# A two-layer streaming trunk on one core: the first chunk of the first layer in a fixed order on four engines

## The chip, the cores and the metric

The kernel runs on one core of one Trainium2 chip. The metric is the device time of one launch in microseconds (us), the median of the runs shown. A core has TensorE (PE in the profile: matmuls, and PEld, its weight loads), VectorE (DVE), ScalarE (ACT), GpSimd (POOL) and SyncE (SP), which here issues the loads. They run their own instruction queues in order and wait for one another by semaphores.

## The reference, cut to what matters

```python
def rmsnorm(x, w):
    x32 = x.astype(jnp.float32)
    y = x32 * lax.rsqrt(jnp.mean(x32 * x32, axis=-1, keepdims=True) + EPS)
    return (y * w.astype(jnp.float32)).astype(x.dtype)

def hybrid_layer(x, layer, norm_w, w_in, ...):
    h = rmsnorm(x, norm_w)
    proj = jnp.einsum('bld,de->ble', h, w_in)
    ...   # forgetting attention, Mamba-2 scan and differential attention on slices of proj,
    ...   # each times a gate and w_branch; merged
    return x + jnp.einsum('bld,de->ble', merged, w_out)
```

There are two layers and a final RMSNorm; x has 256 tokens of 1024 channels. The change lies in `h = rmsnorm(x, norm_w)` of the first layer and in the first 512 columns of `proj`.

## The kernel before, in words

All matrices are float32. To multiply in PE's faster fp32r format without losing precision, each operand is split into a high part (rounded to fp32r) and a low part (the rest), and a product is three matmuls: high by high, high by low, low by high. Weights come packed in chunks of 512 columns (one of 272, one of 272 with small columns); a chunk is four *units* of two 128-row blocks each (`UNITS`, `KU`). For each unit SP issues one load into a `raw` tile (four buffers, `wraw`), ACT casts it to the high part (`whi`, L231) and DVE subtracts to get the low part (`wlo`, L232); after that the raw buffer is free for the load of a later unit. `load_chunk` (L215) does this, and `prefetch` (L914) calls it chunk by chunk.

h is computed by token half `tt` (128 tokens). Squares with a sum go to ACT (L942) and DVE (L944); `norm_scale` (L206) adds four partial sums, `rstd_of` scales (DVE, L181) and raises to the power -0.5 on POOL (L183). `norm_apply` (L210) multiplies x by the token's factor and by the norm weight in one DVE instruction for each half of 512 channels, `c`; the norm weight is a row copied to all 128 partitions by two loads (`load_nwb`, `spread`, L291). `split_rows` (L195) turns h: four PE transposes (L198) put 4 blocks of 128 channels into one PSUM bank, channels now on partitions, and `split_bank` splits it two blocks at a time into `hT` high (ACT, L188) and low (DVE, L189).

`bform` (L240) is a product for one token half with 512 (or 272) output columns, 24 matmuls (L249); `aform` (matmuls L264) has the weights stationary. The first chunk is fv0: its first token half is done with an own order of matmuls, `EARLY` (L237), that takes the passes with the high weights of units 1 to 3 before the one with the low weights; its second half, the chunk fv1 and so on follow. 24 transposes of the identity (`WARM`, L930) run first.

The order of instructions on each engine is set by a planner, which simulates the program with its own costs, takes program order as priority, and puts what stands in `tc.high_priority(URGENT)` first. `tc.issue_after(ins)` puts instructions of ins's engine behind ins. In the opening the loads are issued as x's first half (two), the norm weight (two), two weight units, x's second half (two), two weight units, then the parameters of both layers. At most eight loads are out at a time in the order of issue.

Of the kernel before, what the change touches and what calls it, by code (L numbers as in the profile page):

```python
# [11 lines left out]
F32 = mybir.dt.float32  # L12
F32R = mybir.dt.float32r
# [4 lines left out]
P = 128  # L18
# [14 lines left out]
BUDGET = 3.0  # L33
URGENT = 3000
WARM = 24
BEHIND = 1
ACTSQ = (2, 4)


def rope_tables():  # L40
# [46 lines left out]
    return flat  # L87


def pack_small(conv_w, conv_b, ssm_norm_w, subln_w):  # L90
    rows = np.concatenate([conv_w.reshape(DEPTH, 64, P), conv_b.reshape(DEPTH, 16, P),
                           ssm_norm_w.reshape(DEPTH, 8, P), subln_w.reshape(DEPTH, 1, P)], axis=1)
    return np.ascontiguousarray(rows.transpose(0, 2, 1))


# [1 line left out]
def trunk(ctx: ExitStack, tc: tile.TileContext, x, norm_w, weights, small, vectors,  # L97
# [21 lines left out]
    def rows():  # L119
        return [a2([P, 512]) for _ in range(2)]  # L120
# [7 lines left out]
    def bank(pool, name):  # L128
        return pool.tile([P, 512], F32, name=name)
# [21 lines left out]
    def load_params(l):  # L151
        d = par[l]
        lam_init = 0.8 - 0.6 * math.exp(-0.3 * l)
        pT = const.tile([P, 89], F32, name=f"pT{l}")
        nc.sync.dma_start(pT, small[l])
# [56 lines left out]

    chunks, _ = chunk_list()

    def load_chunk(off, total, after=None, behind=()):  # L215
        units = []
        for u in range(UNITS):
            raw = wraw.tile([P, KU * 512], F32, name="raw")[:, 0:KU * total]
            o = off + u * KU * P * total
            ins = nc.sync.dma_start(raw, weights[o:o + KU * P * total].rearrange("(p f) -> p f", p=P)).ins  # L220
            if u == BEHIND:
                for late in behind:
                    tc.add_manual_dep(late, ins.name, mybir.DependencyInfo(
                        mybir.DependencyClass.NoSync, mybir.DependencyReason.DATA), reason="order")
            hi = wsp.tile([P, KU * 512], F32R, name="whi")[:, 0:KU * total]
            lo = wsp.tile([P, KU * 512], F32R, name="wlo")[:, 0:KU * total]
            with ExitStack() as es:
                if u > 0 and after:
                    for ins in after:
                        es.enter_context(tc.issue_after(ins))  # L230
                S.copy(out=hi, in_=raw)  # L231
                V.tensor_tensor(out=lo, in0=raw, in1=hi.bitcast(F32), op=ALU.subtract)  # L232
            units.append(tuple(t.rearrange("p (k n) -> p k n", k=KU) for t in (hi, lo)))
        return units, total

    ORDER = [(u, k, i) for u in range(UNITS) for k in range(KU) for i in range(3)]
    EARLY = [(u, k, i) for u, i in ((0, 0), (0, 1), (0, 2), (1, 0), (1, 2), (1, 1),  # L237
                                    (2, 0), (2, 2), (2, 1), (3, 0), (3, 2), (3, 1)) for k in range(KU)]

    def bform(ch, act, tt, order=ORDER):  # L240
        units, n = ch
        ahi, alo = act
        ps = bank(pp, "pp")
        for u, k, i in order:
# [4 lines left out]
            PE.matmul(ps[:, 0:n], lhsT=at(a, kt)[:, ts], rhs=w[:, k, 0:n],  # L249
                      start=((u, k, i) == order[0]), stop=((u, k, i) == order[-1]))  # L250
        return ps

    def aform(ch, act, jj):
# [31 lines left out]
    def load_nwb(l):  # L285
        L[l]["nwb"] = spread(norm_w[l])
# [624 lines left out]
    queue = list(chunks)  # L911
    loaded = []

    def prefetch(n, after=None, behind=()):  # L914
        while queue and n > 0:
            l_, k_, _, off, m = queue.pop(0)
            loaded.append((l_, k_, load_chunk(off, m, after, behind)))
            n -= 1

    constants()  # L920
    xt = [rows() for _ in range(2)]

    def load_x(tt):
        for c in range(2):
            cs = slice(512 * c, 512 * c + 512)
            yield nc.sync.dma_start(xt[tt][c], x[0, tt * P:(tt + 1) * P, cs]).ins

    warm = bank(pq, "pq")
    for i in range(WARM):
        PE.transpose(warm[:, (i % 4) * P:(i % 4 + 1) * P], ident, ident)  # L930

    list(load_x(0))
    load_nwb(0)
    x1 = list(load_x(1))
    for tt in range(2):
        xs, ss = rows(), sm.tile([P, 4], F32, name="ss")
        with tc.high_priority(URGENT):
            for q in range(4):
                qs = slice(256 * (q % 2), 256 * (q % 2) + 256)
                a, b = xs[q // 2][:, qs], xt[tt][q // 2][:, qs]  # L940
                if q < ACTSQ[tt]:
                    S.activation(out=a, in_=b, func=AF.Square, accum_out=ss[:, q:q + 1])  # L942
                else:
                    V.tensor_tensor_reduce(out=a, in0=b, in1=b, scale=1.0,  # L944
                                           scalar=0.0, op0=ALU.mult, op1=ALU.add, accum_out=ss[:, q:q + 1])
        g = make_h(0, tt, xt[tt], xs, ss, 1)
        next(g)
        if tt == 0:
            for _ in g:
                pass  # L950
            prefetch(1, [i.ins for i in L[0]["split"]], x1)
            prefetch(1)
        else:
            jobs.append([g, 1])
    for idx, it in enumerate(items):
        if it["key"] == "dq0" and it["l"] == 0:
            with tc.issue_after(L[0]["split"][0].ins), tc.issue_after(L[0]["split"][1].ins):
                load_params(1)
            nc.sync.dma_start(rot, rope_t)
        if it["pre"]:  # L960
            it["pre"]()
        l = it["l"]
        if it["wait"]:
            n = 0
            while it["wait"] not in L[l]:
                assert jobs
                pump(100.0)
                n += 1
            if n > 1:
                print("forced", l, it["key"], n)  # L970
        prefetch(it["n"])
        got = [loaded.pop(0) for _ in range(it["n"])]
        assert got[0][:2] == (l, it["key"]), (got[0][:2], it["key"])
        if idx == 0:
            ch, act = got[0][2], it["act"]()
            it["evac"][0](0, bform(ch, act, 0, EARLY))
            while "h1" not in L[0]:
                pump(BUDGET)
            it["evac"][0](1, bform(ch, act, 1))
            pump(BUDGET)  # L980
            got, it["evac"] = got[1:], it["evac"][1:]
            with tc.issue_after(L[0]["split"][0].ins), tc.issue_after(L[0]["split"][1].ins):
# [37 lines left out]
```

## Time and profile before

| | us |
|---|---|
| median of 3 runs (range) | 955.47 (955.02 to 956.32) |
| profiled execution, its own time | 956.56 |
| span of that execution | 954.8 |
| PE, PEld busy | 942.0, 843.5 |
| DVE, ACT, POOL busy | 700.9, 599.3, 36.3 |
| mean granted TensorE clock | 0.993 |

The profile shows one execution on the core. Busy time is the sum of an engine's instructions without overlaps; PE's matmuls are pipelined, so the time from one start to the next says more than the length of one. The granted clock is a share of 2.4 GHz: 1.00 or 0.50 (1.2 GHz). Idle time stands with the instruction that ended it and with what released it. L followed by a number is a line of the kernel.

### The profile page before, as it was taken

To read this page: it belongs to the slowest core of one execution; us is meant where nothing else is said; L and a number is where in the kernel's file an instruction comes from. 1 tells how busy PE (TensorE), PEld (TensorE's weight loads), DVE (VectorE), ACT (ScalarE), POOL (GpSimd) and SP (SyncE) were. 2 spreads that over 40 slices of the span, in tenths; PEclk is the share of its full clock that TensorE was granted. 3 is DMA by queue.
4 is the path that set the end of the run, shared out by engine and by line. 5 is a ranking of instruction groups with operands and counts; after the bars stand their busy time and mean duration, and the time that the engine had idled before them with its cause. 6 is when DMAs were issued, how large, how long until landed. Compare 5 with 4: busy or idle time off the path is not lost.

```text
span 954.8 us, 16246 instructions
## 1 busy us (share of the span) xinstructions
PE 942.0 (99%) x5924; PEld 843.5 (88%) x5924; DVE 700.9 (73%) x1434; ACT 599.3 (63%) x1141; POOL 36.3 (4%) x71
## 2 busy tenths in 40 slices
PE   7999999999999999999999999999999999999997
PEld 5999999988898988888889989898889999888885
DVE  5678677987667877864768768699777677797463
ACT  4668686654557868653546859566536596975442
POOL 1001100000000000100000110000000000010000
PEclk7999999999999999999999999999999999999999
DMA  6866634575555555555558664456645555555551
GB/s 231 263 219 198 206 101 166 159 226 154 177 189 181 182 190 179 151 171 194 193 181 271 209 206 134 132 172 191 201 143 194 174 186 186 188 158 162 177 188 44
DMA packets 60319, 172.45 MB, mean 181 GB/s; under 512 B 7312, under 2 KB 15824, under 8 KB 60240
## 3 DMA queue, kind: packets, MB, share of 16 engines
q1 hardware_dynamic: 60240, 171.43, 55.4%
q8 instruction: 46, 0.75, 0.3%
q14 instruction: 33, 0.27, 0.1%
HBM read 167.14 MB, written 2.16 MB: 177 GB/s over the span
## 4 chain that ended last, share of the span: by engine, by line
PE 98%; DMA 1%; DVE 1%; ACT 0%; SPq 0%; POOLq 0%; issue 0%
PE pp L249 51%; PE pp L264 34%; PE pq L400 2%; PE pt L457 2%; PE pq L583 1%; PE pq L401 1%; PE pq L447 1%; DMA raw<-in_weights_dram 1%; PE pt L627 1%; PE pt L198 1%; PE pt L458 1%; PE pq L692 1%; PE pq L590 0%; PE pt L700 0%; PE pq L499 0%; PE pt L699 0%
## 5 line engine op out<-in xcount | busy, mean ns | idle before, releaser
L249 PE MATMUL pp<-whi,a 128*128 128x512 f32 (+1 forms) x1472 | 452.5, 387 | 1.9 <-ACT a L188 1.1
L232 DVE TENSOR_TENSOR wlo<-raw,whi 128x1024 fp32r<-128x1024 f32 (+1 forms) x296 | 349.8, 1193 | 82.8 <-ACT whi L231 80.0
L231 ACT CAST whi<-raw 128x1024 fp32r<-128x1024 f32 (+1 forms) x296 | 302.2, 1027 | 135.2 <-PE pp L249 72.3
L264 PE MATMUL pp<-a,whi 128*128 128x256 f32 x1792 | 332.8, 284 | 0.0
L249 PEld LDWEIGHTS pp<-whi,a 128*128 128x128 f32 x1472 | 273.0, 189 | 55.3 <-ACT a L188 1.7
L264 PEld LDWEIGHTS pp<-a,whi 128*128 128x128 f32 x1792 | 281.5, 191 | 1.7 <-issue 1.4
L249 PE MATMUL pp<-wlo,a 128*128 128x512 f32 (+1 forms) x736 | 281.5, 385 | 0.0
L264 PE MATMUL pp<-a,wlo 128*128 128x256 f32 x896 | 255.2, 285 | 0.0
L264 PEld LDWEIGHTS pp<-a,wlo 128*128 128x128 f32 x896 | 171.5, 191 | 1.4 <-issue 1.4
L249 PEld LDWEIGHTS pp<-wlo,a 128*128 128x128 f32 x736 | 138.9, 189 | 25.8 <-DVE wlo L232 0.5
L183 POOL TENSOR_TENSOR rstd<-rstd,mhalf 128x2 f32<-128x2 f32 (+2 forms) x26 | 18.9, 727 | 760.6 <-DVE rstd L181 739.7
L473 DVE SCALAR_TENSOR_TENSOR a<-sw,pT,a 128x255 f32<-128x255 f32 (+2 forms) x96 | 41.8, 477 | 8.1 <-ACT a L470 7.9
L406 ACT ACTIVATE sc<-sc,dnm 128x128 f32<-128x128 f32 x64 | 28.6, 450 | 8.4 <-DVE dnm L403 8.3
L188 ACT CAST a<-pt 128x256 fp32r<-128x256 f32 x32 | 11.5, 371 | 33.2 <-PE pt L198 27.0
L400 PE MATMUL pq<-a,a 128*128 128x128 f32 (+1 forms) x128 | 31.8, 283 | 0.0
L809 DVE SCALAR_TENSOR_TENSOR a<-a,pp 128x512 f32<-128x512 f32 x24 | 16.4, 682 | 20.9 <-PE pp L249 20.9
L401 PE MATMUL pq<-a,a 128*128 128x128 f32 (+1 forms) x128 | 31.5, 269 | 0.0
L406 ACT ACTIVATE sc<-sc,nm 128x128 f32<-128x128 f32 (+1 forms) x64 | 28.5, 447 | 1.3 <-DVE nm L403 1.1
L400 PEld LDWEIGHTS pq<-a,a 128*128 128x128 f32 x128 | 23.7, 191 | 0.3
L401 PEld LDWEIGHTS pq<-a,a 128*128 128x128 f32 x128 | 23.6, 191 | 0.3
L403 DVE CUSTOM_DVE_ANT_0 sc<-pq,sc 128x128 f32<-128x128 f32 (+1 forms) x64 | 19.5, 351 | 5.9 <-POOL sc L426 4.9
L191 ACT ACTIVATE a<-pt,pT 128x256 fp32r<-128x256 f32 x32 | 14.9, 473 | 14.1 <-PE pt L627 12.4
(161 smaller groups left out, 842.6 us busy)
## 6 DMA issues: line engine op xcount, KB each, us to landing
raw<-in_weights_dram SPq DMA_DIRECT2D x280, 512.0 KB, 4.5
raw<-in_weights_dram SPq DMA_DIRECT2D x16, 272.0 KB, 3.5
sc<-scr SPq DMA_DIRECT2D x16, 256.0 KB, 5.5
a<-scr SPq DMA_DIRECT2D x16, 256.0 KB, 5.6
a<-in_x_dram SPq DMA_DIRECT2D x8, 256.0 KB, 5.2
sc<-scr SPq DMA_DIRECT2D x16, 128.0 KB, 5.2
a<-in_norm_w_dram SPq DMA_DIRECT2D x4, 256.0 KB, 6.5
rp<-a SPq DMA_DIRECT2D x32, 32.0 KB, 4.1
```

Of the source, the lines that this page charges most:

```text
L183: G.tensor_tensor(out=r[:, 0:width], in0=r[:, 0:width], in1=mhalf[:, 0:width], op=ALU.pow)
L231: S.copy(out=hi, in_=raw)
L232: V.tensor_tensor(out=lo, in0=raw, in1=hi.bitcast(F32), op=ALU.subtract)
L249: PE.matmul(ps[:, 0:n], lhsT=at(a, kt)[:, ts], rhs=w[:, k, 0:n], start=((u, k, i) == order[0]), stop=((u, k, i) == order[-1]))
L264: PE.matmul(ps[:, j * T:(j + 1) * T], lhsT=w[:, k, c0:c0 + P], rhs=at(a, kt), start=(kt == 0 and j == 0 and i == 0), stop=(kt == KT - 1 an ...
L400: PE.matmul(ps[:, o:o + n], lhsT=q[:, j, qs], rhs=k[:, j, 0:n], start=True, stop=False)
L401: PE.matmul(ps[:, o:o + n], lhsT=q[:, j, qs], rhs=kl[:, j, 0:n], start=False, stop=True)
L403: V.tensor_tensor_reduce(out=sc[:, sl], in0=ps[:, sl], in1=bias[:, sl], scale=-0.125, scalar=BIG, op0=ALU.add, op1=ALU.min, accum_out=nm[: ...
L406: S.activation(out=sc[:, sl], in_=sc[:, sl], func=AF.Exp, scale=-1.0, bias=nm[:, t:t + 1], accum_out=rs[:, t:t + 1])
L457: PE.matmul(po[r, 0:T], lhsT=v0, rhs=pTs[i][:, 0:T], start=True, stop=False)
L473: V.scalar_tensor_tensor(out=xc[:, s:T], in0=u[:, 0:T - s], scalar=pr["conv"](j, k), in1=xc[:, s:T], op0=ALU.mult, op1=ALU.add)
L809: V.scalar_tensor_tensor(out=t, in0=t, scalar=1.0, in1=ps, op0=ALU.add, op1=ALU.mult)
```

## The change

The opening is written out in one function, `opening()`, inside `tc.manual_schedule` for PE, ACT, DVE and SP, which keeps program order on these four queues instead of the planner's. In it:

- The norm weight of the first layer comes as `wcol`, 8 values per partition (channel on partition), packed behind the small parameters. The two row loads are gone for the first layer; the second layer is as before.
- The loads are issued as x's first half, `wcol`, weight units 0 and 1, x's second half, units 2 and 3.
- The multiplication of x takes the token's factor alone: on DVE for the first token half, on POOL and ACT (512 channels each) for the second, whose four squares are all on ACT.
- `split_k` splits the turned h by blocks of 128 channels and multiplies by `wcol` there: high on ACT (on DVE for the first two blocks), low on DVE.
- Splits of weight units, h blocks and the matmuls of fv0's first token half are interleaved unit by unit. PE gets 8 (`FILL`) and three times 4 (`HOLD`) more transposes of the identity between them.
- The parameters and the second chunk's casts and subtractions stand behind the last split of the second token half. `load_chunk` is cut into three helpers; the `EARLY` order and the manual dependence of loads go.

The core of the diff:

```diff
+    def opening():
+        _, _, _, off, n = queue.pop(0)
...
+        def split_k(tt, ps, k, hi_on=S):
+            pk, ts = ps[k // 4][:, k % 4 * P:(k % 4 + 1) * P], slice(tt * P, (tt + 1) * P)
+            h, o, w = at(hT[0], k)[:, ts], at(hT[1], k)[:, ts], wcol[:, k:k + 1]
+            if hi_on is S:
+                hi = S.activation(out=h, in_=pk, func=AF.Copy, scale=w)
+            else:
+                hi = V.tensor_scalar(out=h, in0=pk, scalar1=w, scalar2=None, op0=ALU.mult)
+            lo = V.scalar_tensor_tensor(out=o, in0=pk, scalar=w, in1=h.bitcast(F32),
+                                        op0=ALU.mult, op1=ALU.subtract)
+            return hi.ins, lo.ins
+
+        def passes(u, *forms):
+            for i in forms:
+                for k in range(KU):
+                    kt = u * KU + k
+                    a, w = ((0, his), (0, los), (1, his))[i]
+                    PE.matmul(first, lhsT=at(hT[a], kt)[:, 0:P], rhs=per_k(w[u])[:, k, :],
+                              start=(u == 0 and i == 0 and k == 0), stop=(u == 3 and i == 1 and k == 1))
...
+            load_x(0)
+            nc.sync.dma_start(wcol, small[0, :, 89:97])
+            raw = [load_raw(off, n, u) for u in range(2)]
+            load_x(1)
+            raw += [load_raw(off, n, u) for u in range(2, 4)]
+            keep_warm(WARM)
             for q in range(4):
+                square(0, q, q < 2)
+            r = norm_scale(ss[0])
+            p0 = []
+            for c in range(2):
+                V.tensor_scalar(out=xs[0][c], in0=xt[0][c], scalar1=r[:, 0:1], scalar2=None, op0=ALU.mult)
+                p0.append(turn(0, c))
+            keep_warm(FILL)
+            his[0] = split_hi(raw[0], n)
+            for k in (0, 1):
+                split_k(0, p0, k, V)
+            passes(0, 0, 2)
+            keep_warm(HOLD)
+            los[0] = split_lo(raw[0], his[0], n)
+            for k in (2, 3):
+                split_k(0, p0, k)
+            his[1] = split_hi(raw[1], n)
+            passes(1, 0, 2)
+            keep_warm(HOLD)
+            los[1] = split_lo(raw[1], his[1], n)
+            passes(0, 1)
+            for k in (4, 5):
+                split_k(0, p0, k)
+            for q in range(4):
+                square(1, q, True)
+            his[2] = split_hi(raw[2], n)
+            r = norm_scale(ss[1])
+            passes(2, 0, 2)
+            keep_warm(HOLD)
+            los[2] = split_lo(raw[2], his[2], n)
+            passes(1, 1)
+            for k in (6, 7):
+                split_k(0, p0, k)
+            his[3] = split_hi(raw[3], n)
+            G.tensor_scalar(out=xs[1][0], in0=xt[1][0], scalar1=r[:, 0:1], scalar2=None, op0=ALU.mult)
+            S.activation(out=xs[1][1], in_=xt[1][1], func=AF.Copy, scale=r[:, 0:1])
+            passes(3, 0, 2)
+            los[3] = split_lo(raw[3], his[3], n)
+            passes(2, 1)
+            p1 = [turn(1, 0)]
+            passes(3, 1)
+            p1.append(turn(1, 1))
+            for k in range(8):
+                tail = split_k(1, p1, k)
...
+            it["evac"][0](0, ps0)
+            it["evac"][0](1, bform(ch0, it["act"](), 1))
+            it["n"], it["evac"] = it["n"] - 1, it["evac"][1:]
+            with tc.issue_after(tail[0]), tc.issue_after(tail[1]):
+                prefetch(it["n"])
                 load_params(0)
```

## Rows read from the trace of the kernel before

**Rows 1.** The page, part 4: the chain that ended last, by engine.

```profile
...
PE 98%; DMA 1%; DVE 1%; ACT 0%; SPq 0%; POOLq 0%; issue 0%
...
```

**Rows 2.** Busy time by engine, TensorE clock granted, DMA share, GB/s, 23 to 940 us.

```profile
...
23.00:940.00 917.00, 917.00 (x5828) 824.02 (x5827) 685.52 (x1404) 584.99 (x1107) 32.79 (x55) 1.00 0.56 181
...
```

**Rows 3.** Chain of waits in order of time, 0 to 60 us: start, length, what.

```profile
...
2.65 7.64 DMA raw<-in_weights_dram
...
22.70 18.28 PE pp L249 x122
...
```

**Rows 4.** Timeline of the opening: start, length, engine, line, operation, count, idle before.

```profile
...
1.70 0.91 SPq L291 DMA_DIRECT2D a<-in_norm_w_dram  x2
...
4.45 0.43 DVE L944 CUSTOM_DVE_ANT_0 a<-a 128x256 f32<-128x256 f32 x1 [4.45 <-DMA a<-in_x_dram]
...
6.81 0.75 DVE L210 SCALAR_TENSOR_TENSOR a<-a,rstd,a 128x512 f32<-128x512 f32 x1 [1.13 <-DMA a<-in_norm_w_dram]
...
9.05 0.75 DVE L210 SCALAR_TENSOR_TENSOR a<-a,rstd,a 128x512 f32<-128x512 f32 x1 [1.49 <-DMA a<-in_norm_w_dram]
...
14.44 1.99 ACT L231 CAST whi<-raw 128x1024 fp32r<-128x1024 f32 x2
...
15.52 2.36 DVE L232 TENSOR_TENSOR wlo<-raw,whi 128x1024 fp32r<-128x1024 f32 x2 [0.52 <-ACT whi L231]
...
```

**Rows 5.** Stretches of the opening, columns as in rows 2.

```profile
...
4.00:4.50 0.50, 0.50 (x4) 0.50 (x4) 0.05 (x1) 0.50 (x3) 0.00 (x0) 1.00 0.54 180
7.00:9.50 2.50, 0.83 (x6) 0.42 (x4) 1.01 (x2) 0.00 (x0) 0.00 (x0) 1.00 0.91 370
10.50:11.00 0.50, 0.12 (x1) 0.00 (x0) 0.00 (x0) 0.50 (x1) 0.00 (x0) 0.50 1.08 430
17.00:20.50 3.50, 3.50 (x10) 2.73 (x9) 2.60 (x6) 3.17 (x9) 0.56 (x1) 0.50 0.59 164
20.50:21.00 0.50, 0.50 (x4) 0.41 (x3) 0.50 (x2) 0.01 (x1) 0.00 (x0) 0.98 0.03 9
...
```

**Rows 6.** Timeline of TensorE: transposes at 2 and 22 us, matmuls at 440 us.

```profile
...
2.03 5.18 PE L930 MATMUL pq<-ident 128*128 128x128 f32 x24 [2.03 <-POOL mhalf L147]
...
21.64 1.03 PE L198 MATMUL pt<-ident,a 128*128 128x128 f32 x8
...
439.96 0.39 PE L249 MATMUL pp<-wlo,a 128*128 128x512 f32 x1
440.19 0.61 PE L249 MATMUL pp<-whi,a 128*128 128x512 f32 x2
...
```

**Rows 7.** Groups by line and shape: count, busy us, mean ns; last, min/median/max ns.

```profile
...
L232 DVE TENSOR_TENSOR wlo<-raw,whi 128x544 fp32r<-128x544 f32 x16 | 11.3, 722 | 7.5 <-ACT whi L231 7.5
...
L707 DVE SCALAR_TENSOR_TENSOR a<-pt,rstd,a 128x128 f32<-128x128 f32 x32 | 9.7, 344 | 5.3 <-POOL rstd L183 5.3
...
L614 DVE TENSOR_SCALAR a<-a,rstd 128x256 f32<-128x256 f32 x16 | 4.5, 348 | 2.3 <-POOL rstd L183 2.3
...
L171 DVE TENSOR_TENSOR br<-br 128x128 f32<-128x128 f32 x2 | 0.6, 282 | 0.0
...
L191 ACT ACTIVATE a<-pt,pT 128x256 fp32r<-128x256 f32 x32 | 14.9, 473 | 14.1 <-PE pt L627 12.4 <-DVE a L192 1.4
...
L183 POOL TENSOR_TENSOR rstd<-rstd,mhalf 128x4 f32<-128x4 f32 x4 | 4.1, 1018 | 325.0 <-DVE rstd L181 325.0
L183 POOL TENSOR_TENSOR rstd<-rstd,mhalf 128x1 f32<-128x1 f32 x6 | 3.3, 558 | 174.0 <-DVE rstd L181 174.0
...
masks.py:199 POOL TENSOR_SCALAR_AFFINE_SELECT ident<-ident 128x128 f32<-128x128 f32 x1 | 0.3, 298 | 0.0
...
L426 POOL TENSOR_SCALAR_AFFINE_SELECT sc<-sc x32: 403/409/1475, 70.1 to 570.2; 128x256 f32<-128x256 f32 x32
...
```

**Rows 8.** Timeline at 95 us: a select on POOL beside a weight split on DVE.

```profile
...
95.67 1.22 DVE L232 TENSOR_TENSOR wlo<-raw,whi 128x1024 fp32r<-128x1024 f32 x1
...
95.68 1.48 POOL L426 TENSOR_SCALAR_AFFINE_SELECT sc<-sc 128x256 f32<-128x256 f32 x1 [1.12 <-DMA sc<-scr]
...
```

More of the change, by code (lines that the diff above doesn't have):

```diff
@@ L213, in trunk, with load_raw, split_hi @@
     chunks, _ = chunk_list()
-    def load_chunk(off, total, after=None, behind=()):
+    def load_raw(off, total, u):
+        raw = wraw.tile([P, KU * 512], F32, name="raw")[:, 0:KU * total]
+        o = off + u * KU * P * total
+        nc.sync.dma_start(raw, weights[o:o + KU * P * total].rearrange("(p f) -> p f", p=P))
+        return raw
+    def split_hi(raw, total):
+        hi = wsp.tile([P, KU * 512], F32R, name="whi")[:, 0:KU * total]
+        S.copy(out=hi, in_=raw)
+        return hi
@@ L221, in load_chunk @@
[L221 to L232, printed above, removed]
@@ L240, in bform @@
-    def bform(ch, act, tt, order=ORDER):
+    def bform(ch, act, tt):
         units, n = ch
@@ L243, in bform @@
         ps = bank(pp, "pp")
-        for u, k, i in order:
+        for u, k, i in ORDER:
             whi, wlo = units[u]
@@ L912, in trunk, with prefetch @@
     loaded = []
-    def prefetch(n, after=None, behind=()):
+    def prefetch(n):
         while queue and n > 0:
             l_, k_, _, off, m = queue.pop(0)
-            loaded.append((l_, k_, load_chunk(off, m, after, behind)))
+            loaded.append((l_, k_, load_chunk(off, m)))
             n -= 1
     constants()
[L921 to L937, printed above, removed]
-            for q in range(4):
[L939 to L954, printed above, removed]
+    def opening():
+        _, _, _, off, n = queue.pop(0)
+        st = L[0]
+        xt = [rows() for _ in range(2)]
+        xs = [rows() for _ in range(2)]
+        ss = [sm.tile([P, 4], F32, name="ss") for _ in range(2)]
+        hT = st["hT"] = halves()
+        wcol = const.tile([P, 8], F32, name="wcol")
+        warm = bank(pq, "pq")
+        first = bank(pp, "pp")
+        def keep_warm(m):
+            for i in range(m):
+                PE.transpose(warm[:, (i % 4) * P:(i % 4 + 1) * P], ident, ident)
+        def load_x(tt):
+            for c in range(2):
+                nc.sync.dma_start(xt[tt][c], x[0, tt * P:(tt + 1) * P, 512 * c:512 * c + 512])
+        def square(tt, q, on_act):
+            qs = slice(256 * (q % 2), 256 * (q % 2) + 256)
+            a, b = xs[tt][q // 2][:, qs], xt[tt][q // 2][:, qs]
+            if on_act:
+                S.activation(out=a, in_=b, func=AF.Square, accum_out=ss[tt][:, q:q + 1])
+            else:
+                V.tensor_tensor_reduce(out=a, in0=b, in1=b, scale=1.0,
+                                       scalar=0.0, op0=ALU.mult, op1=ALU.add, accum_out=ss[tt][:, q:q + 1])
+        def turn(tt, c):
+            ps = bank(pt, "pt")
+            for j in range(4):
+                PE.transpose(ps[:, j * P:(j + 1) * P], xs[tt][c][:, j * P:(j + 1) * P], ident)
+            return ps
+        def split_k(tt, ps, k, hi_on=S):
[3 more added lines that the diff above has]
+                hi = S.activation(out=h, in_=pk, func=AF.Copy, scale=w)
+            else:
+                hi = V.tensor_scalar(out=h, in0=pk, scalar1=w, scalar2=None, op0=ALU.mult)
[9 more added lines that the diff above has]
+                              start=(u == 0 and i == 0 and k == 0), stop=(u == 3 and i == 1 and k == 1))
+        his, los, r = {}, {}, {}
+        with tc.manual_schedule(engines={mybir.EngineType.PE, mybir.EngineType.Activation,
+                                         mybir.EngineType.DVE, mybir.EngineType.SP}):
+            load_x(0)
[4 more added lines that the diff above has]
+            keep_warm(WARM)
+            for q in range(4):
+                square(0, q, q < 2)
+            r = norm_scale(ss[0])
+            p0 = []
+            for c in range(2):
+                V.tensor_scalar(out=xs[0][c], in0=xt[0][c], scalar1=r[:, 0:1], scalar2=None, op0=ALU.mult)
[37 more added lines that the diff above has]
+                tail = split_k(1, p1, k)
+        st["h0"] = st["h1"] = True
+        return ([(per_k(his[u]), per_k(los[u])) for u in range(UNITS)], n), first, tail
@@ L970, in trunk @@
                 print("forced", l, it["key"], n)
-        prefetch(it["n"])
-        got = [loaded.pop(0) for _ in range(it["n"])]
-        assert got[0][:2] == (l, it["key"]), (got[0][:2], it["key"])
         if idx == 0:
[L975 to L982, printed above, removed]
-                load_params(0)
+            it["evac"][0](0, ps0)
+            it["evac"][0](1, bform(ch0, it["act"](), 1))
+            it["n"], it["evac"] = it["n"] - 1, it["evac"][1:]
+            with tc.issue_after(tail[0]), tc.issue_after(tail[1]):
+                prefetch(it["n"])
+                load_params(0)
+            got = [loaded.pop(0) for _ in range(it["n"])]
+        else:
+            prefetch(it["n"])
+            got = [loaded.pop(0) for _ in range(it["n"])]
+            assert got[0][:2] == (l, it["key"]), (got[0][:2], it["key"])
         for s in range(2):
```

32 lines of the change are left out of this document (18 added, 14 removed).

## The prediction

> **What bounds the kernel now.** I read the chain of waits first, then busy time by stretch, then the timeline of the first 24 us. The chain is TensorE (PE) for 98% [rows 1]: the kernel is one long queue of matmuls. From 23 to 940 us PE is busy in all of the 917 us and at the full clock, while VectorE (DVE, 685 us) and ScalarE (ACT, 585 us) have slack [rows 2]. So nothing is to be had there; what can move is the moment from which PE has no more gaps. In the chain in order of time that moment is the hand-over at 22.70 us, the first matmul of the second token half; before it the chain is a DMA until 10.29 us (2.65 + 7.64) and then short pieces of ACT, DVE and PE [rows 3]. Everything PE does after the hand-over is the same in both kernels: 24 matmuls of fv0 for the second token half and all later chunks. The sum is therefore 22.70 minus the new hand-over, and whether PE stays without gaps after it.
>
> Why is the hand-over so late? Two reasons. First the loads: the two norm-weight loads (each 256 KB, one row copied to 128 partitions) are issued at 1.70 us, ahead of the weights. DVE waits for them twice, until 6.81 and 9.05 us [rows 4], and while they run the DMA engines move 180 GB/s, against 430 later [rows 5]. Second the clock. The 24 warm-up transposes take 5.18 us, 0.21 apart, although the clock column already reads 1.00 there; eight transposes at 21.6 us take 1.03 us, 0.11 apart [rows 6]. So the full clock came only near the end of the warm-up. Then PE works 0.83 us of the 2.5 from 7.0 to 9.5, the clock falls to 0.50 by 10.5, and it is back at 20.5 us, after PE was busy for all of 17.0 to 20.5 [rows 5]. Most of the 24 matmuls of the first token half so ran at 1.2 GHz: 512 columns in 0.43 us, against 0.23 from start to start at the full clock [rows 6].
>
> **The change part by part.** I carry the four queues forward by hand. Back to back, the next start comes some 0.08 us before an end: two DVE weight splits of 1.22 us [rows 8] take 2.36 together, two ACT casts 1.99 [rows 4]. So I count 1.14 and 0.95 each, and 0.08 more for the last.
>
> *Loads.* x's first half is issued and lands as before, 4.45 us [rows 4]. The per-channel weights (4 KB, 32 bytes a partition) follow; no row shows so small a load. It costs between 0 and 2.2 us (a norm-weight half: 6.81 to 9.05); I take 0.1, since by bytes it is 1/64 of that half, and nothing waits for it before 7.7. Without the two slow loads a weight unit (0.52 MB) needs 1.25 us at 420 GB/s: unit 0 at 5.8, unit 1 at 7.05, x's second half at 8.3, units 2 and 3 at 9.55 and 10.8. SyncE's nine issues, 0.45 us each [rows 4], end by 5 us and stay ahead. Unit 0 so comes 4.5 us earlier; the other end is 0, if it was not these loads that held the queue.
>
> *Norm of the first half.* Squares and the power on GpSimd (POOL) stay and end at 6.4 us. The multiplication by the row's norm alone costs between 0.35 us (128x256) and 0.75 (128x512 with the weight) [rows 7, 4]; I take 0.49, an estimate nearer to the first row, which is the same operation. The halves are ready at 6.9 and 7.35. The transposes stand behind the warm-up, which ends at 7.2; the banks are ready at 7.7 and 8.1. The 8 fillers run until 8.8.
>
> *Splits.* Eight casts and eight subtractions of 128x256 become 16 and 16 of 128x128 with a scale. One on DVE: 0.34 [rows 7], 0.26 apart. One on ACT: between 0.24 and 0.47 (half and all of a 128x256 with the same kind of scale) [rows 7]; I take 0.36, 0.28 apart. DVE then runs: two channel blocks, high and low, 7.7 to 8.9; unit 0's low part to 10.05; blocks 2 and 3 to 10.55; unit 1 to 11.7; blocks 4 and 5 to 12.2; two small norm steps to 12.5; unit 2 to 13.65; blocks 6 and 7 to 14.15; unit 3 to 15.3. ACT: unit 0's high part 5.8 to 6.9; blocks 2, 3 to 8.4; unit 1 to 9.35; blocks 4, 5 to 9.9; four squares (0.40 each, between the 0.36 of a block and a 0.47) to 11.4; unit 2 to 12.45; blocks 6, 7 to 13.0; unit 3 to 13.95; its half of the second norm to 14.6. By that table DVE and ACT are the bound in the opening, no longer the loads.
>
> *POOL's multiplication (128x512, new).* It starts at 13.5, after the power. Price: no multiplication on POOL is in the trace. Its selects take 0.30 for 128 columns and 0.41 for 256, so 0.63 for 512; its power takes 0.56 for one column and 1.02 for four, which for 512 would be 79 us [rows 7]. I take 0.63: a select is also one simple step per element, a power is not. A select that began beside a DVE weight split took 1.48 us instead of 0.41 [rows 8], so units 2 and 3 on DVE may hold it up; it is then done at 14.2, at the latest at about 15.6.
>
> *PE.* Unit 0's four matmuls 8.8 to 9.75, 4 fillers to 10.2; unit 1's wait for blocks 2, 3 and end at 11.1, fillers to 11.55; unit 0's low part to 12.0; unit 2 waits for ACT until 12.45. From there PE has no wait left: 4 matmuls 0.92, fillers 0.44, two 0.46, four 0.92, two 0.46, four transposes 0.44 (they need POOL's result at 15.65), two 0.46 (they need unit 3's low part, 15.3), four transposes 0.44. That is 4.54, hand-over at 17.0. Behind it the second token half is split on ACT and DVE in 0.28 us steps, while PE needs 0.69 us a block: no wait.
>
> **Sum:** 22.70 - 17.0 = 5.7 us less. The 20 fillers (2.2 us at full clock) stand where PE would wait, except the last hold (0.44), counted. What covers the rest: the second chunk (fv1) is first used 24 matmuls later, at 22.5; its loads wait in SyncE's queue for the raw buffers, which come free at 10 to 15.3 instead of from 12.6 on, and DVE and ACT are rid of the opening at 18.9. One of its units costs 0.72 us on DVE [rows 7], so unit 0 is there at about 19.6 to 21, before 22.5. If that cover fails, PE waits for the difference.
>
> The profiled execution took 956.56 us for a span of 954.8. 956.56 - 5.7 = 950.9; the median of the runs, 955.47, lies 1.1 below it, and from it the same gain gives 949.8. I cannot tell how much of that 1.1 is the opening; I take 950.3.
>
> **The rivals.** (a) *The clock is not held.* PE falls back to 1.2 GHz near 10 us as before. For: it fell in this trace with PE mostly idle before it, and was back only at 20.5 [rows 5]; the table leaves gaps too. Against: none of them is over 0.8 us, and at the lower level PE's work fills them. Price: the 4.54 us from 12.45 on take at most twice that, hand-over at 21.5 and a gain of 1.2; with the full clock back half-way 19.3, gain 3.4. I take the second: 2.3 on the forecast, 952.6.
> The fillers are transposes, and those are weighed here. In the trace nothing but transposes ran before their spacing went from 0.21 to 0.11 us [rows 6]. The Trainium skill (TensorE: Matmul & The Clock Gate, Part 4: PE-mode transpose) says that the full clock does not engage for transposes, because they do not count as busy in the same way. By that rule fillers would hold nothing and rival (a) would be the forecast; the trace does not agree with it, and (a) has the chance that the gaps of the table leave it.
>
> (b) *The gain is given back in the next chunks*, because parameter steps and evacuations on DVE go ahead of fv1's splits. The parameter steps are twelve, of at most 0.28 us [rows 7]; behind 18.9 all of them would bring unit 0 to 23.0, 0.5 late, and two evacuations of a bank to 24: up to 1.5 us of gap, 951.8. Against it: a unit takes 0.72 us on DVE and its six matmuls about as long, so it happens once, and steps that nothing waits for may go later.
>
> (c) *The loads come no earlier*: the queue was slow for another reason. Unit 0 then lands at 10.3 as before, the others 1.25 apart and unit 3 at 15.3; its cast, its low part and the last 0.9 us of PE bring the hand-over to 18.5, 1.5 late: 951.8. For: the first us of a queue may be slow for any load. Against: x, in the same slots, was there by 4.45, and the queue ran at 430 by 10.5 [rows 4, 5].
>
> (d) *Slower: POOL multiplies at the rate of its power.* The second half's first turn waits for it and PE's queue behind it: unit 3's low part, the second turn, all else. It decides from 2.1 us on (13.5 to 15.6), and from 7.8 us on the kernel is slower than before. At 0.15 us a column: 79 us, hand-over 77 later, about 1027 us. For: the only arithmetic on POOL in this trace. Against: the selects, 0.9 ns a column.
>
> (e) *The rest of the program is ordered anew* and loses a few us: it has no gaps now, so it can only lose; with DVE busy 75% [rows 2] I count up to 8 us, 958.
>
> **How the numbers follow.** Forecast 0.62, (a) 0.13, (b) 0.11, (c) 0.06, (d) 0.03, (e) 0.05. The forecast's own hand-over is 16.2 to 18.2 (a twentieth on every step, and the small load up to 1 us late), that is 949.0 to 952.0 with the 1.1 us between profile and median. The range takes in (a), (b) and (c) and an opening a little faster than the table (the loads alone, unit 3 at 10.8 and the 3.2 us behind it, allow 14): 948.2 to 953.7. Less than 0.2% (1.9 us) cannot be told from no change. Faster 0.91, same 0.04 (parts of (b) and (e)), slower 0.05.
>
> **What would show it.** Unit 0's cast on ACT starts before 6.5 us (loads). The clock reads 1.00 throughout 8 to 17 us (fillers). POOL's multiplication takes under 1 us by itself and PE's transposes of the second half do not wait for it. The 24th matmul of the first token half and the last of the turns end near 17 us, and from there PE shows no idle time; 23 to 930 looks as before. It is wrong if the hand-over is after 19 us, or if it is at 17 and the time does not fall by 5.

## The result, and the profile after

The changed kernel takes 964.25 us (median of 6 runs, 961.28 to 965.78) against 955.59 for the kernel before beside it (6 runs, 955.02 to 956.32): a ratio of 1.0085, with a 95% interval of [1.0067, 1.0103]. It is 0.85% slower; 950.3 was forecast, in a range of 948.2 to 953.7. The profiled execution took 964.85 us, with a span of 963.1.

Where that comes from is read with a ledger that the next tables use too: for a matmul of the kernel before, how much earlier (-) or later (+) the other kernel starts the matmul at which it has done the same number of columns (transposes of the identity, which fill time, are left out). After the change TensorE (PE) is 0.35 us late at 28 us, 0.97 at 55, 1.60 at 64, 6.94 at 80, 8.45 at 150 and 8.42 at 900. So the opening gained nothing, and some 7 us more went between 60 and 150 us, where [rows 2] had no gap. A ledger compares one execution of each kernel, and these lie up to 1.3 us beside the median of their kernel, so a difference of less than about 1 us between two ledgers says little.

Stretches of the kernel after (PE, PEld, DVE, ACT and POOL busy, granted clock, DMA share, GB/s). The third answers to [rows 2]:

```profile
...
10.50:11.00 0.50, 0.28 (x3) 0.04 (x1) 0.41 (x2) 0.06 (x1) 0.00 (x0) 1.00 1.01 390
17.00:20.50 3.50, 3.31 (x12) 2.27 (x12) 2.48 (x4) 1.92 (x3) 2.39 (x1) 0.65 0.31 80
...
23.00:940.00 917.00, 913.87 (x5791) 820.26 (x5790) 683.47 (x1402) 585.60 (x1103) 31.62 (x54) 1.00 0.57 181
77.00:80.00 3.00, 0.63 (x5) 0.43 (x4) 1.24 (x9) 1.13 (x5) 1.26 (x4) 0.91 0.73 220
80.00:86.30 6.30, 6.30 (x30) 6.30 (x31) 6.07 (x25) 6.30 (x20) 4.40 (x7) 0.50 0.75 250
...
```

The clock is no longer down at 10.5 as in [rows 5], but it falls at 18, for 3.4 us, and a second time at 79.5, for 6.8 us, behind a stretch in which PE worked 0.63 us of 3.

Timeline of the opening after (start, length, engine, line, operation, count, idle before and its releaser); it answers to [rows 3, 4]:

```profile
...
7.09 1.05 ACT L223 CAST whi<-raw 128x1024 fp32r<-128x1024 f32 x1 [2.74 <-DMA raw<-in_weights_dram]
...
9.43 1.22 DVE L228 TENSOR_TENSOR wlo<-raw,whi 128x1024 fp32r<-128x1024 f32 x1
9.60 0.37 ACT L963 ACTIVATE a<-pt,wcol 128x128 fp32r<-128x128 f32 x1 [1.46 <-DVE a L966]
...
10.57 0.34 DVE L966 SCALAR_TENSOR_TENSOR a<-pt,wcol,a 128x128 fp32r<-128x128 f32 x1
...
10.95 0.37 ACT L963 ACTIVATE a<-pt,wcol 128x128 fp32r<-128x128 f32 x1 [0.97 <-DVE a L966]
11.21 1.03 ACT L223 CAST whi<-raw 128x1024 fp32r<-128x1024 f32 x1
...
12.30 1.20 PE L975 MATMUL pp<-whi,a 128*128 128x512 f32 x4 [1.51 <-ACT whi L223]
...
15.66 1.03 ACT L223 CAST whi<-raw 128x1024 fp32r<-128x1024 f32 x1
...
16.86 2.53 POOL L1021 TENSOR_SCALAR a<-a,rstd 128x512 f32<-128x512 f32 x1
...
18.51 1.03 ACT L223 CAST whi<-raw 128x1024 fp32r<-128x1024 f32 x1
...
23.19 0.47 PE L252 MATMUL pp<-whi,a 128*128 128x512 f32 x1
...
24.31 0.37 ACT L963 ACTIVATE a<-pt,wcol 128x128 fp32r<-128x128 f32 x1 [0.42 <-DVE a L966]
...
24.71 0.35 DVE L966 SCALAR_TENSOR_TENSOR a<-pt,wcol,a 128x128 fp32r<-128x128 f32 x1 [0.43 <-ACT a L963]
...
25.09 0.62 ACT L963 ACTIVATE a<-pt,wcol 128x128 fp32r<-128x128 f32 x2 [0.42 <-DVE a L966]
...
27.97 2.27 ACT L223 CAST whi<-raw 128x544 fp32r<-128x544 f32 x4
...
29.12 0.72 DVE L228 TENSOR_TENSOR wlo<-raw,whi 128x544 fp32r<-128x544 f32 x1
...
```

Waits of the whole kernel after (us in total, times, longest):

```profile
...
ACT a L963 <- DVE a L966: 7.1, 9, 1.5
...
DVE a L966 <- ACT a L963: 6.2, 10, 2.2
...
```

The two rows of waits are the finding. ScalarE (ACT) writes a block's high part, VectorE (DVE) its low part; that DVE waits for ACT is in the arithmetic. But ACT also waits for DVE: block 3's high part at 10.95 begins only behind block 2's low part (10.57), which has nothing to do with it except that both are read from the same turned bank. In the tail (from 24.31 on) the blocks so stand some 0.79 us apart. And it is the bank that is read, not the tile written: block 2 at 24.31 opens a new tile of the output and waits all the same, while at 25.09 ACT does two blocks in one go, and the second of them is the first of the next bank. (Each bank is one tile of the program here, so whether the bank counts or the tile that fills it, no run tells.) I call this the lockstep. The Trainium skill (PSUM — Partial Sum Buffer, PSUM bank collisions raise a hardware error) says that a compiler's scheduler puts a dependency between any two instructions of different engines that touch the same 32-partition quadrant of one bank, ScalarE and VectorE as two readers too. The rows agree, since all of these instructions span 128 partitions; what put the order in here, they do not show.

In the opening the lockstep costs more than 0.79, because a 1.22 us weight split stands between a high part and its low part in DVE's queue (9.43): blocks 2 and 3 hold ACT from 9.60 to 11.21, and unit 1's cast behind them starts at 11.21. PE waits 1.51 us for it.

### The profile page after: what moved, and what is told of

Same layout as the page of the kernel before. It is cut to its first block, busy times and chain, and to the rows that moved or that the text cites. A ratio compares the mean times of both kernels' runs of the same rounds, so it can differ in the third digit from the quotient of the medians.

```text
span 963.1 us, 16304 instructions
## 1 busy us (share of the span) xinstructions
PE 947.1 (98%) x5944; PEld 847.6 (88%) x5944; DVE 700.5 (73%) x1442; ACT 602.1 (63%) x1148; POOL 38.2 (4%) x72
## 4 chain that ended last, share of the span: by engine, by line
PE 91%; issue 7%; POOL 0%; DVE 0%; DMA 0%; POOLq 0%; SPq 0%; DVEq 0%
PE pp L252 48%; PE pp L267 31%; PE pq L403 2%; PE pt L460 2%; PE pq L586 1%; PE pq L404 1%; PE pq L450 1%; PE pt L630 1%; PE pt L461 1%; PE pt L198 1%; PE pq L695 1%; PE pq L593 0%; PE pt L701 0%; PE pq L502 0%; PE pt L703 0%
## 5 line engine op out<-in xcount | busy, mean ns | idle before, releaser
L252 PE MATMUL pp<-whi,a 128*128 128x512 f32 (+1 forms) x1456 | 443.1, 384 | 0.0
L252 PEld LDWEIGHTS pp<-whi,a 128*128 128x128 f32 x1456 | 269.0, 188 | 52.1 <-ACT a L963 0.7
L252 PEld LDWEIGHTS pp<-wlo,a 128*128 128x128 f32 x728 | 136.8, 188 | 25.4 <-DVE wlo L228 0.6
L403 PE MATMUL pq<-a,a 128*128 128x128 f32 (+1 forms) x128 | 33.3, 291 | 2.4 <-DVE nm L406 2.4
L404 PE MATMUL pq<-a,a 128*128 128x128 f32 (+1 forms) x128 | 32.4, 277 | 0.0
L188 ACT CAST a<-pt 128x256 fp32r<-128x256 f32 x24 | 8.7, 369 | 30.5 <-PE pt L198 26.5
L406 DVE CUSTOM_DVE_ANT_0 sc<-pq,sc 128x128 f32<-128x128 f32 (+1 forms) x64 | 19.6, 351 | 9.0 <-POOL sc L429 8.0
L192 DVE SCALAR_TENSOR_TENSOR a<-pt,pT,a 128x256 fp32r<-128x256 f32 x32 | 14.7, 479 | 13.4 <-ACT a L191 12.9
```

The source lines that it names most:

```text
L403: PE.matmul(ps[:, o:o + n], lhsT=q[:, j, qs], rhs=k[:, j, 0:n], start=True, stop=False)
L404: PE.matmul(ps[:, o:o + n], lhsT=q[:, j, qs], rhs=kl[:, j, 0:n], start=False, stop=True)
L406: V.tensor_tensor_reduce(out=sc[:, sl], in0=ps[:, sl], in1=bias[:, sl], scale=-0.125, scalar=BIG, op0=ALU.add, op1=ALU.min, accum_out=nm[: ...
```

## The experiments

Twelve kernels were run beside the kernel before, whose median was 956.21 to 956.27 then (955.59 beside the kernel after). "Lead" is the ledger at 28, 55, 80 and 900 us (minus: earlier than before).

| kernel | us, median | ratio to before, 95% | lead at 28 / 55 / 80 / 900 us |
|---|---|---|---|
| after | 964.25 | 1.0085 [1.0067, 1.0103] | +0.35 / +0.97 / +6.94 / +8.42 |
| a_grouped | 952.96 | 0.9966 [0.9953, 0.9979] | -4.47 / -4.55 / -2.82 / -2.55 |
| a_free | 956.94 | 1.0007 [0.9998, 1.0017] | -0.46 / -0.07 / -0.06 / +0.54 |
| a_nofill | 965.51 | 1.0093 [1.0075, 1.0111] | +1.11 / +1.23 / +6.46 / +8.14 |
| a_pool | 963.02 | 1.0068 [1.0051, 1.0085] | -0.61 / -0.01 / +5.72 / +7.48 |
| a_gn | 952.82 | 0.9965 [0.9951, 0.9978] | -4.08 / -4.16 / -3.33 / -3.32 |
| a_gq | 952.86 | 0.9967 [0.9955, 0.9980] | -5.05 / -5.13 / -3.86 / -3.38 |
| a_gf | 952.42 | 0.9961 [0.9948, 0.9975] | -4.30 / -4.42 / -3.89 / -3.83 |
| a_gqf | 951.94 | 0.9958 [0.9945, 0.9970] | -5.29 / -5.32 / -4.56 / -4.55 |
| b_wcol | 951.80 | 0.9956 [0.9943, 0.9968] | -4.69 / -4.64 / -4.64 / -4.60 |
| b_wlock | 956.46 | 1.0000 [0.9991, 1.0009] | -1.19 / -1.34 / -1.01 / -1.11 |
| b_wload | 955.90 | 0.9995 [0.9987, 1.0004] | -1.57 / -1.54 / -0.78 / -0.70 |
| b_grouped | 954.50 | 0.9986 [0.9977, 0.9995] | -1.60 / -1.67 / -0.72 / -0.74 |

**a_grouped: the lockstep taken away**, by order alone; same instructions, same work (blocks 4, 5 and 6, 7 as 2, 3).

```diff
-            for k in (2, 3):
-                split_k(0, p0, k)              # high 2, low 2, high 3, low 3
+            split_ks(0, p0, (2, 3))            # high 2, high 3, low 2, low 3
...
-            for k in range(8):
-                tail = split_k(1, p1, k)
+            for c in range(2):
+                tail = split_ks(1, p1, range(4 * c, 4 * c + 4))
```

> The changed kernel, with the splits of the turned h in another order: first the high parts of a pair (ACT, two in a row), then its low parts (DVE, two in a row); for the second token half in fours, bank by bank. Nothing else differs. Theory A (ACT and DVE take turns on one PSUM bank: each high part waits for the low part before it, and that one stands behind a 1.22 us weight split on DVE; in the changed kernel 16 such turns cost 7.1 and 6.2 us of waiting): the turns go, the casts of units 1 to 3 come 2 to 4 us earlier, the hand-over to the second token half falls from 23.2 to 18 to 20 us, and the time by 3 to 5 us, to about 960; more if the stall at 77 us goes with it. Rival (the opening is late for its loads, its half clock or POOL's 2.5 us multiplication): hand-over within 1 us of 23.2, time unchanged.

Timeline of a_grouped: the casts of units 1 to 3, the first half of the tail, the hand-over and DVE's first subtraction of fv1.

```profile
...
9.39 1.05 ACT L223 CAST whi<-raw 128x1024 fp32r<-128x1024 f32 x1
...
12.44 1.04 ACT L223 CAST whi<-raw 128x1024 fp32r<-128x1024 f32 x1
...
13.89 1.07 ACT L223 CAST whi<-raw 128x1024 fp32r<-128x1024 f32 x1
...
17.49 1.14 ACT L966 ACTIVATE a<-pt,wcol 128x128 fp32r<-128x128 f32 x4 [1.92 <-PE pt L956]
...
18.11 0.47 PE L252 MATMUL pp<-whi,a 128*128 128x512 f32 x1
...
21.71 0.72 DVE L228 TENSOR_TENSOR wlo<-raw,whi 128x544 fp32r<-128x544 f32 x1
...
```

The casts come at 9.39, 12.44 and 13.89 instead of 11.21, 15.66 and 18.51; four high parts take 1.14 us; the hand-over is at 18.11 instead of 23.19. The clock reads 1.00 from 6.15 us to 948. 11.3 us of time go, which is more than the loss: with the lockstep the kernel is slower than before, without it 0.34% faster. Not all of the 11.3 is lost at the lockstep itself, as the next run shows.

**a_free: the second loss.** In the changed kernel the casts and subtractions of the second chunk (fv1) are tied behind the last split of the opening. Here only the tie is taken away; the lockstep stays.

```diff
-            with tc.issue_after(tail[0]), tc.issue_after(tail[1]):
-                prefetch(it["n"])
+            prefetch(it["n"])
+            with tc.issue_after(tail[0]), tc.issue_after(tail[1]):
                 load_params(0)
```

> The changed kernel, but casts and subtractions of the second chunk are no longer tied behind the last split of the second token half; the planner may put them between. Theory B (the second chunk's weights are late because they wait behind the opening, and the later delay, the 2.65 us wait of PE at 77 us with its 6.8 us at half clock, is this lateness handed on): the gap of 0.5 to 0.9 us at 29 us goes, DVE has two weight units more done at 44 us, the wait at 77 us shrinks below 1 us and the time falls by 4 to 7 us to 958 to 960. Rival (the wait at 77 us is a matter of the order that the planner wrote for the softmax part, not of lateness): only the gap at 29 us goes, 963 to 964.

The opening is nearly as late (hand-over 22.71), and still the 7 us between 60 and 150 us are gone: 956.94, better than theory B's 958 to 960. The chain behind them in the kernel after, from its timeline:

```profile
...
63.65 0.26 DVE L357 SCALAR_TENSOR_TENSOR sc_l<-sc_l,br 128x16 f32<-128x16 f32 x2
...
69.45 0.42 SPq L374 DMA_DIRECT2D scr<-sc_cum  x1
...
73.78 0.39 SPq L425 DMA_DIRECT2D sc<-scr  x1
...
78.09 0.41 POOL L429 TENSOR_SCALAR_AFFINE_SELECT sc<-sc 128x256 f32<-128x256 f32 x1 [58.70 <-DMA sc<-scr]
...
79.76 0.47 PE L403 MATMUL pq<-a,a 128*128 128x128 f32 x1 [2.37 <-DVE nm L406]
...
```

The same steps in the kernel before:

```profile
...
58.38 0.26 DVE L354 SCALAR_TENSOR_TENSOR sc_l<-sc_l,br 128x16 f32<-128x16 f32 x2
...
65.96 0.38 SPq L422 DMA_DIRECT2D sc<-scr  x1
...
70.13 0.41 POOL L426 TENSOR_SCALAR_AFFINE_SELECT sc<-sc 128x256 f32<-128x256 f32 x1 [51.07 <-DMA sc<-scr]
...
```

And in a_free:

```profile
...
59.33 0.26 DVE L357 SCALAR_TENSOR_TENSOR sc_l<-sc_l,br 128x16 f32<-128x16 f32 x2
...
```

DVE's first subtraction of fv1 starts at 29.12 us (before 21.56, in a_free 20.40). At sc_l it has done 24 weight splits in all three kernels, and it gets there 5.3 us later than before, against 0.95 in a_free. From there a write to DRAM, loads, a select and a maximum follow; the first of the loads is 7.8 us later, and PE, which was itself only 1.6 late, waits 2.37 us and then runs 6.8 us at half clock, which costs some 3.4 (an estimate: half of it, as PE is busy throughout). PE's own wait for fv1 at 29 us was 0.4. The price of the tie was not paid where it was put.

The two losses hang together, as a square of four kernels shows: 964.25 with lockstep and tie, 956.94 with the lockstep alone, 952.96 with the tie alone, 952.42 with neither (a_gf, below). The lockstep alone costs 4.5 us; the tie alone 0.5, which cannot be told from nothing; both together 11.8. The tie is dear only where the lockstep makes the tail late: DVE's first subtraction of fv1 starts at 29.12 with both, at 21.71 in a_grouped, which has the tie too, and at 21.56 before.

**a_nofill** (`FILL, HOLD = 0, 0` in the kernel after) **and a_gn** (the same in a_grouped): what do the fillers do?

> The changed kernel without its 20 filler transposes; the 24 at the start stay. If the fillers hold the clock, it falls to 0.50 soon after 10 us as in the kernel before and the matmuls of the first token half run at half speed: hand-over 1 to 3 us later, time 1 to 3 us longer. If they do not hold it (the changed kernel fell to 0.50 at 18 us with them), the hand-over stays within 0.7 us of 23.2 and the time within 1 us.

> The changed kernel with the grouped order of the splits and without the fillers (FILL and HOLD at 0). Theory A (the lockstep made the gaps; without it the fillers are needed no longer): the gaps of TensorE between 8.4 and 14.6 us stay as short as in the grouped kernel, the granted clock stays 1.00, and the time is 953.0 us (952.5 to 953.4). Rival C (the fillers hold the clock in themselves): the clock is 0.50 for 3 to 7 us somewhere between 8 and 24 us as in the kernel without fillers alone, which costs half of that, hand-over at 19.5 to 21.5, and the time is 954.5 to 956.5 us.

With the lockstep the clock is at half for 6.8 us of the opening without fillers (from 17.3 us, not soon after 10), instead of 3.4 with them, and PE is 0.8 us later at 28 (hand-over 24.28); the time, 965.51 (963.22 to 966.53), can't be told from 964.25. Without the lockstep the clock holds by itself:

```profile
...
8.00:17.00 9.00, 6.12 (x27) 4.14 (x25) 7.74 (x16) 7.74 (x19) 3.08 (x2) 1.00 0.83 289
...
```

That is a_gn, columns as above: PE busy 6.12 us of 9, clock 1.00, and the time is that of a_grouped. Without the lockstep the fillers are worth nothing that the time shows.

**a_pool:** GpSimd's multiplication on DVE, in the kernel after.

```diff
-            G.tensor_scalar(out=xs[1][0], in0=xt[1][0], scalar1=r[:, 0:1], ...)
+            V.tensor_scalar(out=xs[1][0], in0=xt[1][0], scalar1=r[:, 0:1], ...)
```

> The changed kernel, with the multiplication of the second token half's first 512 channels on DVE in place of POOL (0.44 us for 128x512 there against 2.53 us). Theory A: POOL's result is ready at 19.4 us and first used by the transposes at 21.9, so nothing is gained: hand-over 22.5 to 24, time within 1 us of the changed kernel. Rival (POOL's 2.5 us delays DVE or PE): hand-over 1 to 2 us earlier, 1 to 2 us shorter.

```profile
...
18.31 0.48 DVE L1021 TENSOR_SCALAR a<-a,rstd 128x512 f32<-128x512 f32 x1
...
```

0.48 us there against 2.53 on GpSimd. The median is 1.2 us lower, within the spread of the kernel after; the wait for nm stays (2.7 us). The hand-over was nearly 1 us earlier (22.26), outside theory A's range, but 0.6 us of that stood already at unit 1's cast (10.61 for 11.21), before any multiplication of the second half; and the 7 us behind were lost all the same.

**b_wcol: the weight part alone.** The kernel before, its own order by the planner, no fillers behind the first 24 transposes, no GpSimd multiplication; only the norm weight moves to the split (and the two row loads go), the splits grouped.

```diff
-    load_nwb(0)
+    nc.sync.dma_start(wcol, small[0, :, 89:97])
...
+        for k in range(4 * c, 4 * c + 4):
+            h = S.activation(out=at(hi, k)[:, ts], in_=ps[...], func=AF.Copy, scale=w[:, k:k + 1])
+        for k in range(4 * c, 4 * c + 4):
+            o = V.scalar_tensor_tensor(out=at(lo, k)[:, ts], in0=ps[...], scalar=w[:, k:k + 1], ...)
```

> The kernel before with the weight part of the change alone: the norm weight per channel at the split (four copies, then four subtractions per bank), the two norm-weight row loads replaced by the 4 KB load; order by the planner, no fillers, no GpSimd multiplication. Theory L (the loads set the opening): the weight units land about 3 us earlier, the hand-over comes near 20.0 instead of 22.70, time 953.3 us (952.5 to 954.2). Rival O (the order of the queues sets it): the loads are earlier, but the planner's order of casts and splits uses less than 1 us of that, or TensorE's clock falls for longer, time 955 to 956.5 us.

Timeline of b_wcol, and its stretches from 23 to 940 and from 8 to 17 us:

```profile
...
6.70 1.05 ACT L246 CAST whi<-raw 128x1024 fp32r<-128x1024 f32 x1 [2.43 <-DMA raw<-in_weights_dram]
...
7.65 2.17 ACT L202 ACTIVATE a<-pt,wcol 128x128 fp32r<-128x128 f32 x8
...
8.92 2.15 DVE L205 SCALAR_TENSOR_TENSOR a<-pt,wcol,a 128x128 fp32r<-128x128 f32 x8
...
17.92 0.50 PE L264 MATMUL pp<-whi,a 128*128 128x512 f32 x1 [0.60 <-ACT a L202]
...
```

```profile
...
23.00:940.00 917.00, 917.00 (x5818) 823.57 (x5817) 682.37 (x1393) 584.17 (x1104) 33.33 (x55) 1.00 0.56 181
8.00:17.00 9.00, 7.26 (x29) 4.52 (x30) 7.42 (x16) 7.69 (x22) 0.56 (x1) 1.00 0.89 319
...
```

Better than either theory: 951.80, the lowest median of all that ran, and 0.44% faster than before. Eight high parts take 2.17 us and eight low parts 2.15, 0.26 apart: about the figures that my table had used. The clock reads 1.00 from 5.2 us to 947, without fillers, where the kernel before is at half from 10.3 to 20.5; how much of the gain goes by way of the clock was not separated. The lead of 4.6 us stands to the end without a gap. The opening written out in a fixed order was not needed for it.

**b_wlock: the same with the lockstep**, that is, high and low of each block in turn.

> The kernel before with the weight part alone, but with the order of the changed kernel in each bank: copy, subtraction, copy, subtraction. Theory A (the lockstep costs wherever the order has it): the pairs stand 0.6 to 0.8 us apart instead of 0.28, the second bank's splits end 2 to 3 us later, hand-over near 20 to 21 instead of 17.92, time 954.0 us (953.2 to 956). Rival P (the planner fills the gaps between the pairs with other work, so that nothing is lost): 951.8 to 952.4.

Waits of b_wlock, 4 to 30 us:

```profile
...
PE pp L263 <- ACT whi L245: 4.0, 1, 4.0
ACT a L202 <- DVE a L204: 2.4, 5, 0.9
...
```

956.46: the whole gain of the weight part is gone; rival P is refuted. The lockstep costs 4.7 us under the planner (956.46 - 951.80) and about the same in the fixed order without the tie (956.94 - 952.42 = 4.5); the 11.3 of after and a_grouped have the tie in them.

**b_wload: the loads kept.** b_wcol with `load_nwb(0)` still in its place, its rows unused.

> The kernel before with the weight part alone and grouped splits, but the two row loads of the norm weight are kept where they were, and their rows are not used. Theory L (the gain of the weight part is the loads' place in the queue): unit 0 lands at about 10.6 again instead of 6.7, hand-over at 22 to 23.5, time 955.5 us (954.8 to 957). Rival W (the gain is that VectorE no longer waits for the rows and multiplies by a scalar): the first turns stay at 6.7 and the hand-over comes before 20.5, 952.5 to 954.

```profile
...
10.81 1.04 ACT L246 CAST whi<-raw 128x1024 fp32r<-128x1024 f32 x1 [6.52 <-DMA raw<-in_weights_dram]
...
12.18 1.22 PE L264 MATMUL pp<-whi,a 128*128 128x512 f32 x2 [3.83 <-ACT a L202]
...
```

```profile
...
8.00:17.00 9.00, 5.17 (x15) 3.52 (x14) 4.74 (x12) 6.19 (x19) 0.09 (x1) 0.66 0.96 354
...
```

Unit 0's cast is back at 10.81, the clock is at half again for a part of 8 to 17 us, and the time is 955.90: theory L. (The first matmul of the second token half, at 19.64, stands here before eight of the first half's 24, so it is no hand-over to compare; the lead is 1.57 us at 28.) Of b_wcol's 4.4 us, 4.1 are the loads' place in the queue (the 4 KB load, which stands there in addition, is counted in). That b_wload gains less than b_grouped below, which has the loads and the grouping too, was not settled; their intervals overlap.

**b_grouped: grouping alone**, in the kernel before (two high halves of a bank, then the two low ones).

> The kernel before with one edit: each turned bank is split by both ScalarE copies first and both VectorE subtractions behind them, instead of copy, subtraction, copy, subtraction. Theory A (the lockstep is there in the kernel before too, and short): each bank's second copy starts at once behind the first instead of 0.35 us later, the hand-over comes 0.3 to 0.7 us earlier than 22.70, time 955.1 us (954.8 to 955.5). Rival: the lockstep is hidden there behind the weight loads, 955.6 us, no difference.

954.50, better than expected. In its profiled execution, at 955.80 one of the slower ones, the lead is 1.6 us at 28, and 0.9 of it is lost again, most of that in one wait of 0.66 us for nm before 67.6 us. So the lockstep was there in the kernel before; it shows there as well, in its waits from 4 to 30 us and its timeline:

```profile
...
ACT a L188 <- DVE a L189: 1.9, 2, 1.4
...
```

```profile
...
12.53 0.42 DVE L189 TENSOR_TENSOR a<-pt,a 128x256 fp32r<-128x256 f32 x1
...
12.98 0.65 ACT L188 CAST a<-pt 128x256 fp32r<-128x256 f32 x2 [1.35 <-DVE a L189]
...
```

**a_gf, a_gq, a_gqf: how far the fixed order goes.** a_gf is a_grouped without the tie; a_gq is a_grouped with unit 2's cast ahead of the squares of the second token half, two of those on DVE, and the multiplication on DVE; a_gqf has both.

> The changed kernel with the grouped order of the splits and with the casts and subtractions of fv1 not tied behind the last split. Theory B (the rest of what the opening gains is lost where fv1 comes late behind the tail and VectorE is then late with the small chain): hand-over 18.1 as in the grouped kernel, the waits for sc_l at 56 and for nm at 68 and 74 us go, and a lead of 4.4 us stands to the end: 951.4 us (951.0 to 952.0). Rival O (these waits come from the planner's order of VectorE in fq1 and fk, however fv1 is tied): 952.6 to 953.2, as in the grouped kernel.

> The changed kernel with the grouped order of the splits, the multiplication of the second token half's first half on VectorE instead of GpSimd, unit 2's cast ahead of the squares of the second token half, and two of those squares on VectorE. Theory A (what is left in the opening is set by the order written for ScalarE and VectorE): unit 2's cast starts near 11.1 instead of 12.44, TensorE's wait of 0.95 us at 13.54 goes, the hand-over comes at about 17.0 instead of 18.11, and the time is 952.0 us (951.6 to 952.4). Rival B (the chunk behind can't use it): hand-over near 17.0 too, but the waits for sc_l and nm at 56, 68 and 74 us grow by the same 1.1 us, and the time stays at 952.7 to 953.2.

> The same freeing of fv1 on top of the reordered opening (grouped, multiplication on VectorE, squares behind unit 2's cast). Theory B: lead of 5.0 us at 24 us, kept to the end, 950.9 us (950.5 to 951.5). Rival O: the wait for nm near 73 us stays, 952.5 to 953.0.

a_gq is 0.6 us ahead of a_grouped at 28 us (not 1.1), and 0.8 at 900, but its time, 952.86, is the same: rival B by the time, while the ledgers are too close to say where it went (a_grouped's is of its slowest execution, 953.89). a_gf has a lead of 3.83 at 900 where a_grouped had 2.55, but its time is only 0.5 lower, with overlapping intervals. Together, 951.94: between theory B's 950.9 and rival O's 952.5, and level with b_wcol. Why some of the lead goes in these three kernels, in waits of 0.2 to 0.4 us for sc_l and nm, and none in b_wcol, was not settled.

## Why the prediction was wrong

**The step that failed is Splits.** It put high and low parts into two queues that each run on their own, 0.28 and 0.26 us apart, and took casts at 8.4, 11.4 and 13.0 from that. The durations were right (0.37 and 0.35 us by themselves, 0.26 back to back for both), but in the order of the change the two engines wait for each other at most of the blocks. The casts came at 11.21, 15.66 and 18.51. The hand-over came at 23.19, not 17.0. Grouped, the same table holds to about 1 us: 9.39, 12.44, 13.89, hand-over 18.11. The rows of before under b_grouped would have told: ACT waiting for DVE on a bank that both only read. I read the chain of waits, where it hardly shows, and not the list of waits.

**"What covers the rest" failed too, and by a longer way than I had priced.** I had fv1 on DVE at 19.6 to 21 and wrote that PE waits for the difference if the cover fails. It began at 29.12 because it is tied behind the tail, and PE waited 0.4 us. But what stands behind fv1 on DVE came later with it, sc_l by 5.3 us, and 7 us were lost at 64 to 150 us. The cover fails because the lockstep makes the tail late: in a_grouped, tied as well, fv1 begins at 21.71. Rival (b) is the nearest to this mechanism, with 1.5 us at most; (e) had the size (958, up to 8 us) without the mechanism. Neither reached the 964 that both losses make.

**The sum:** 22.70 is no full counterpart of the new hand-over. In the kernel before only 22 of the first half's 24 matmuls stand ahead of it, and two follow at 23.39 and 23.62; the same table was thus worth some 0.5 us more than the 5.7 that I wrote. This does not touch what failed.

**Loads:** the direction was right, 1.3 us too early. Unit 0's cast starts at 7.09, not 5.8, so the first test of the prediction (before 6.5) failed; unit 3 lands at 12.3, not 10.8. Unit 0 lands at 7.07 instead of 10.29 [rows 3], 3.2 us earlier, and b_wload shows that this is nearly all the gain there is. (c) is refuted.

**GpSimd's multiplication:** 2.53 us, four times the 0.63 taken from the selects; still far from (d)'s 79. The sign "under 1 us" failed, yet the time is hidden (done at 19.39, used at 21.94), as the a_pool runs say.

**The clock:** 1.00 from 8 to 17 us, as forecast, but not because of the fillers, and it fell right after, when PE had waited 1.5 and 2.35 us. So rival (a) came in part, at 18 us and not near 10, as a consequence of the lockstep: in a_grouped and in a_gn the clock does not fall.

## What to carry to other kernels

Where two engines read one bank, look in the list of waits for the pair A <- B and B <- A before pricing their queues apart, and let one engine finish its reads of the bank before the other begins. Price a tie by what it delays on its in-order engine, down to the next place where PE needs something from there, not by the first wait. And run the smallest part of a change by itself: here one load and the splits in groups of four did at least as well as any opening written out by hand.

## What the runs showed of the hardware that I had not expected

GpSimd takes 2.53 us for a 128x512 multiplication by a column, 5.3 times DVE's 0.48 for the same line; it was 2.52 or 2.53 in every profile that has it. A load of 4 KB in 32-byte rows is not always free: in the kernel after it lands 1.0 us behind x's first half (5.08 after 4.05 us), and between 0.2 (b_wlock) and 1.8 us (a_grouped) in the others. In the kernel after, GB/s in 40 slices of 0 to 6 us:

```profile
...
GB/s 0 0 0 0 0 0 0 0 0 0 0 0 177 205 150 232 341 396 423 410 382 388 248 138 17 29 56 57 173 301 382 247 300 273 300 300 355 382 328 355
...
```

17 to 57 GB/s in the four slices from 3.6 to 4.2 us, against 423 at 2.7 and 382 at 4.5. I had counted 0.1 for it. Whether it is what made my loads 1.3 us too early is not shown: in a_free it lands only 0.27 us behind x, and unit 0's cast still starts at 6.98 there, against 7.09.
